# Making half of the second layer's modulation vectors in the token choice of the first expert layer instead of in the even mixer

## The chip, the cores and the metric

The program runs on one core of one Trainium2 chip. The metric is the device time of one execution in microseconds (us); the table further down gives the median of three runs. PE is TensorE with its matmuls, PEld its loading of weights, DVE VectorE, ACT ScalarE, POOL GpSimd and SP SyncE, whose queue issues most of the transfers. Numbers such as L926 are lines of the kernel before.

## What is computed

The reference is a first block (attention, gated recurrence, projections) and behind it two layers of a second block. Each layer of the second block needs six vectors per stream, made from a small input and one wide matrix, and ends in an expert layer that picks its tokens. Cut to what the change touches:

```python
for i in range(DEPTH_2):                                        # two layers
    mod = jnp.einsum('bd,de->be', jax.nn.silu(c), ada_w[i]) + ada_b[i]
    mod_c = jax.nn.silu(c_ctx) @ ada_w[i] + ada_b[i]
    sh1, sc1, g1, sh2, sc2, g2 = jnp.split(mod[:, None, :], 6, -1)
    ...
    h = rms_norm_2(x, norm1_g[i]) * (1.0 + sc1) + sh1           # norm 1
    y, yc = even_mixer(h, hc, ...)  if i % 2 == 0 else odd_mixer(h, hc, ...)
    x = x + g1 * y
    h = rms_norm_2(x, norm2_g[i]) * (1.0 + sc2) + sh2           # norm 2
    x = x + g2 * expert_choice_ffn(h, moe_router[i], moe_w1[i], moe_w3[i], moe_w2[i])

def expert_choice_ffn(h, router, w1, w3, w2):
    ...
    gate, idx = lax.top_k(jnp.swapaxes(aff, 1, 2), cap)         # 16 experts choose cap tokens each
    xs = jax.vmap(lambda hb, ib: hb[ib])(h, idx)
    hid = jax.nn.silu(jnp.einsum('becd,edf->becf', xs, w1)) * jnp.einsum('becd,edf->becf', xs, w3)
    ys = jnp.einsum('becf,efd->becd', hid, w2) * gate[..., None]
    ...                                                         # added back to the chosen rows
```

`x` has 512 rows and the context 256 rows of 1024 numbers; `ada_w` is 2 x 1024 x 6144, all in 32-bit floats.

## The kernel before

**The vectors.** `Mods.make(psum, p, w, ahead, part)` is a generator that makes the vectors of one layer. Part 0 makes `sh1` and `sc1`, part 1 the other four. It walks over pieces of `ada_w` of 512 rows by 128 columns. Each step of part 1, of which there are 64, loads one piece into a tile `aw` (256 KB, rows of 512 B; the load is L903, in a ring of `ahead` + 1 buffers) and multiplies it on PE (L926, four matmuls in the program, eight in the trace). After each eighth step ACT copies the sums (L931, tile `aev`), and one step later PE turns them (L910) and DVE adds the bias (L911). In front stand two small loads of the bias and the norm's gain into `aev` with a transpose (L240, L244), behind stand the gates' transposes (L942), a copy (L943) and a store (L944, to `mg`).

**The even mixer.** It starts with a gated stage (four column blocks, each of 512- and 256-column matmuls in three terms, L102 to L104, on weights that a `Feed` loads, splits on ACT into `whi` and on POOL into `wlo`, L184 to L201). Its results (`glu`, L1143 and L1144) feed a convolution of 31 taps per block. Three of the four blocks run on DVE, one instruction a tap (L1098, L1100, tile `acc`). Then come the low-rank projections: per row tile ACT squares (L1162), DVE and POOL make the norm (L110, L115), DVE scales (L1164), PE turns (L1178), ACT and DVE split (L1182, L1183). After them come attention and the output projection. The generator `both` is stepped between the matmuls of the gated stage and of the low-rank stage.

**The token choice.** `first.run()` is the expert layer of the first layer. Logits of all tokens lie in PSUM (L1517, L1518). `choose` turns them (L1534) and finds the largest eight per pass on DVE (L1544, L1545), eight passes for `x` and four for the context. Then it sums along the rows (L1550), turns (L1554), and `fetch` makes the list of rows (L1470, L1473). POOL gathers them (L1477, tile `xs`). `turn` (L1567) transposes the gathered rows, and with that the experts begin (L1617 up, L1656 down). The experts' weights arrive in 192 tiles `w` of 1 MB over a ring of 14. Eight are issued on SP before the choice, six on POOL behind the gather, the rest on SP as buffers come free.

**The order** of the instructions on each engine is fixed when the program is built: a scheduler orders what the generators emit, and each engine and each queue then works in that order.

Of the kernel before, what the change touches and what calls it, by code (L numbers as in the profile page):

```python
# [218 lines left out]
def setup(k):  # L219
    nc = k.nc  # L220
    k.cp = k.pool("cp", side="left")
    cc = k.cp.tile(list(CONSTS.shape), F32, name="cc")
    k.load_consts = lambda: nc.sync.dma_start(cc, k.i["consts"])
    k.c = {n: cc[:, o:o + w] for n, (o, w) in COFF.items()}
    k.id = k.c["ident"]
    k.mhalf = k.cp.tile([128, 1], F32, name="mhalf")
    nc.vector.memset(k.mhalf, -0.5)
# [631 lines left out]
def ada_setup(k, psum):  # L859

    nc, I = k.nc, k.i
    c1 = columns(k, [("c", I["c_2"].rearrange("a (r p) -> (a r) p", p=128)),
                     ("cc", I["c_ctx_2"].rearrange("(r p) -> r p", p=128))], k.cp, psum)
    k.router = k.cp.tile([128, 2, 8, 16], F32, name="router")
    for layer in range(2):
        nc.gpsimd.dma_start(k.router[:, layer], I["moe_router_2"][layer].rearrange("(k p) e -> p k e", p=128))
    k.cT = k.cp.tile([128, 8, 32], F32, name="cT")
    nc.gpsimd.memset(k.cT, 0.0)
    for r, nm in enumerate(("c", "cc")):
        th = k.cp.tile([128, 8], F32, name="cth" + nm)  # L870
        nc.scalar.activation(th, c1[nm], AF.Tanh, scale=0.5)
        nc.vector.scalar_tensor_tensor(th, th, 1.0, c1[nm], ALU.add, ALU.mult)
        nc.vector.tensor_scalar(k.cT[:, :, r], th, 0.5, None, ALU.mult)
# [558 lines left out]
def moe(k, layer, groups, mods, psum, es, nslot, extra, out=None, side="right"):  # L1432
# [19 lines left out]
    def load(upto, eng=nc.sync):  # L1452

        for i in range(len(W), min(upto, len(todo))):
            e, nm, q = todo[i]
            a = i % (nslot + extra) >= nslot
            w = pools[a].tile([128, 2 * D], F32, name="w", tag="w", bufs=extra if a else nslot).rearrange("p (k f) -> p k f", k=2)
            d = eng.dma_start(w, I[f"moe_{nm}_2"][layer, e][q * 256:q * 256 + 256].rearrange("(k p) f -> p k f", p=128))
            if i < nslot + extra:
                k.tc.keep_in_program_order(d)  # L1460
            W[e, nm, q] = w
# [211 lines left out]
                nc.scalar.copy(t[so], yb[64 * dh + 32:64 * dh + 64])  # L1673
                nc.vector.tensor_tensor(ys[so, ds_], ys[so, ds_], t[so], op=ALU.add)

    def run():
        nonlocal rp, pf, pq, p, iota, tid, one, hb
        slots()
        rp = k.pool(f"mr{layer}", 1, None, es)
# [10 lines left out]
        with ExitStack() as e2:  # L1690
            pq = k.pool(f"mq{layer}", 1, None, e2, "left")
            one = pq.tile([16, 512], F32, name="one")
            nc.gpsimd.memset(one, 1.0)
            chosen = [choose(gi, g) for gi, g in enumerate(G)]
            while any(g is None for g in nxt):
                for c in chosen:
                    next(c, 0)
        load(nslot + extra, nc.gpsimd)
        load(24)
        p = k.pool(f"mx{layer}", 1, None, es)  # L1700
# [879 lines left out]
def whole(tc, I, out):  # L2580
    nc = tc.nc
    with ExitStack() as es:
        k = K(tc, I, es)
        setup(k)
        psum = k.pool("ps", 8, PSUM)
        dr = k.pool("dr", 1, DRAM)
        mp = k.pool("mp", side="left")
        ex = ExitStack()
        mods = [Mods(k, i, mp, dr) for i in range(2)]

        def vectors():

            ada_setup(k, psum)
            with ExitStack() as e2:
                yield from mods[0].make(psum, k.pool("ad", 1, None, e2), 128, 4, 0)

        x = block1(k, lambda: k.pool("xp", 1, None, ex, "left").tile([128, 4, D], F32, name="xres"), psum, vectors)
        c = k.pool("xc", 1, None, ex, "left").tile([128, 2, D], F32, name="cres")
        nc.sync.dma_start(c, I["ctx_2"][0].rearrange("(t p) d -> p t d", p=128))
        xt, ct = [x[:, t] for t in range(4)], [c[:, t] for t in range(2)]  # L2600
        first = moe(k, 0, [(0, xt, 64), (1, ct, 32)], mods[0], psum, ExitStack(), 14, 0, side="left")
        def both(p):
            for a in range(2):
                yield from mods[1].make(psum, p, 128, 6, a)

        even_mixer(k, xt, ct, mods[0], psum, first, both)
        first.run()

        xs = dr.tile([S, D], F32, name="xspill")
        for t in range(4):  # L2610
            nc.sync.dma_start(xs[t * 128:t * 128 + 128], xt[t])

        def open_x():
            x2 = k.pool("xp2", 1, None, es, "left").tile([128, 4, D], F32, name="xres2")
            for t in range(4):
                nc.sync.dma_start(x2[:, t], xs[t * 128:t * 128 + 128])
            return [x2[:, t] for t in range(4)]

        res, last = [None] * 4, ExitStack()
        second = moe(k, 1, [(0, res, 64)], mods[1], psum, last, 11, 9, out[0])  # L2620
        odd_mixer(k, xt, ct, mods[1], psum, ex.close, open_x, second, last, res)
        second.run()
# [26 lines left out]
```

## Time and profile before

| | us |
|---|---|
| median of three runs | 3463.92 |
| lowest and highest of the three | 3454.38, 3468.79 |
| the profiled execution | 3452.15 |
| its span, from the first to the last instruction | 3450.3 |

The profiled execution is 12 us below the median. The span falls into stages, of which two matter here: the gated and low-rank stages of the even mixer, at 1020 to 1150 us, and the token choice of the first expert layer, at 1489 to 1523 us. A busy share is an average over stages with different limits, so each of the two is read by itself: which engine is full in it, and which wait ends last. The profile also gives, for any stretch, the clock that TensorE was granted (1.00 is 2.4 GHz, 0.50 is 1.2 GHz), the busy share of the 16 DMA engines (packets that overlap can bring it over 1) and the rate in GB/s.

### The profile page before, as it was taken

The numbers are of one execution on the slowest core, as the hardware profiler recorded it, in microseconds if no ns is written. First come the engines' busy times: TensorE is split into PE (matmuls) and PEld (weight loads), VectorE is DVE, ScalarE is ACT, GpSimd is POOL, SyncE is SP. The second block draws the span as 40 slices with busy tenths as digits, with TensorE's granted clock in tenths as the row PEclk, the third lists the DMA queues.
The fourth block names the chain that finished last, engine by engine and source line by source line (L and its number), as shares of the span: only waits on it lengthen the run. The fifth ranks groups of instructions, "written<-read, shape, count | busy, mean of one in ns | idle before, by whom it ended". The sixth has DMA issues, their size and how long they took to land.

```text
span 3450.3 us, 52389 instructions
## 1 busy us (share of the span) xinstructions
PE 3103.6 (90%) x21072; PEld 2032.6 (59%) x21072; DVE 1538.3 (45%) x3435; ACT 1013.0 (29%) x2175; POOL 975.3 (28%) x859
## 2 busy tenths in 40 slices
PE   8999999998989899979999999899768579699888
PEld 6898778886768666743333333687647467333322
DVE  3233544414378687342323334331577776332212
ACT  4333333322212454211111212222557443011000
POOL 5342434332323552410000000424646344000000
PEclk9999999999989999979999999899879779899999
DMA  4121122225257232178888884343222234799998
GB/s 145 61 74 49 62 74 70 66 68 166 93 158 203 81 101 65 49 304 339 333 341 334 333 339 166 105 140 117 80 59 71 66 96 154 311 409 409 409 409 349
DMA packets 372552, 625.94 MB, mean 181 GB/s; under 512 B 43998, under 2 KB 240525, under 8 KB 372310
## 3 DMA queue, kind: packets, MB, share of 16 engines
q1 hardware_dynamic: 367190, 603.58, 49.2%
q0 software_dynamic: 5120, 19.01, 1.5%
q8 instruction: 167, 2.74, 0.3%
q14 instruction: 75, 0.61, 0.1%
HBM read 596.61 MB, written 25.91 MB: 180 GB/s over the span
## 4 chain that ended last, share of the span: by engine, by line
PE 73%; DVE 11%; DMA 8%; ACT 4%; issue 2%; POOL 2%; SPq 1%; POOLq 0%; DVEq 0%; ACTq 0%
PE ps L102 11%; PE h L1617 10%; PE ps L103 10%; PE ps L104 10%; PE yb L1656 7%; DMA w<-in_moe_w_dram 6%; PE hc L1617 4%; PE ps L1599 2%; PE ps L926 1%; PE ob L762 1%; PE ps L2253 1%; DVE acc L1100 1%; DVE pr L2308 1%; DVE N L2309 1%; PE ob L1303 1%
## 5 line engine op out<-in xcount | busy, mean ns | idle before, releaser
L201 POOL TENSOR_TENSOR wlo<-wraw,whi 128x1024 fp32r<-128x1024 f32 (+5 forms) x219 | 426.8, 1970 | 755.2 <-ACT whi L197 736.5
L1617 PE MATMUL h<-w,xT 128*64 128x512 f32 x2048 | 462.6, 597 | 23.7 <-DMA w<-in_moe_w_dram 18.1
L1617 PEld LDWEIGHTS h<-w,xT 128*64 128x64 f32 x2048 | 141.1, 137 | 335.0 <-issue 253.9
L1656 PE MATMUL yb<-w,hT 128*64 128x512 f32 (+1 forms) x1536 | 301.0, 599 | 17.8 <-ACT hT L1640 15.4
L197 ACT CAST whi<-wraw 128x2048 fp32r<-128x2048 f32 (+4 forms) x108 | 161.5, 1495 | 235.7 <-PE ps L103 111.8
L1477 POOL DMA_INDIRECT xs<-xh,ii x20 | 21.3, 1067 | 728.9 <-DVE sl L1480 708.6
L1625 DVE SCALAR_TENSOR_TENSOR th<-th,h 128x512 f32<-128x512 f32 x32 | 22.0, 688 | 413.3 <-ACT th L1624 413.3
L1656 PEld LDWEIGHTS yb<-w,hT 128*64 128x64 f32 (+1 forms) x1536 | 87.2, 128 | 197.3 <-issue 153.6
L102 PE MATMUL ps<-hT,whi 128*128 128x512 f32 x416 | 171.2, 412 | 0.0
L102 PE MATMUL ps<-whi,hT 128*128 128x512 f32 (+1 forms) x424 | 164.3, 388 | 4.9 <-DVE hT L316 2.7
L103 PE MATMUL ps<-hT,wlo 128*128 128x512 f32 x416 | 166.3, 400 | 0.0
L1624 ACT ACTIVATE th<-h 128x512 f32<-128x512 f32 x32 | 19.1, 597 | 499.7 <-PE h L1617 499.7
L104 PE MATMUL ps<-hT,whi 128*128 128x512 f32 x416 | 165.7, 398 | 0.0
L103 PE MATMUL ps<-whi,hT 128*128 128x512 f32 (+1 forms) x424 | 156.4, 369 | 0.0
L104 PE MATMUL ps<-wlo,hT 128*128 128x512 f32 (+1 forms) x424 | 154.5, 367 | 0.0
L115 POOL TENSOR_TENSOR rs<-rs_t,mhalf 128x8 f32<-128x8 f32 (+3 forms) x78 | 94.7, 1218 | 113.5 <-DVE rs_t L110 93.7
L1617 PE MATMUL hc<-w,xT 128*32 128x512 f32 x1024 | 124.2, 598 | 0.0
L1669 DVE TENSOR_TENSOR ys<-yb,g 64x512 f32<-64x512 f32 x64 | 44.1, 688 | 177.5 <-PE yb L1656 177.0
L102 PEld LDWEIGHTS ps<-whi,hT 128*128 128x128 f32 x424 | 104.3, 246 | 14.5 <-DVE hT L316 3.2
L103 PEld LDWEIGHTS ps<-whi,hT 128*128 128x128 f32 x424 | 104.6, 247 | 6.4 <-issue 1.9
L1100 DVE SCALAR_TENSOR_TENSOR acc<-glu,w,acc 128x798 f32<-128x798 f32 x90 | 106.6, 1221 | 1.0
L104 PEld LDWEIGHTS ps<-wlo,hT 128*128 128x128 f32 x424 | 103.9, 246 | 5.2 <-issue 0.2
(810 smaller groups left out, 6831.4 us busy)
## 6 DMA issues: line engine op xcount, KB each, us to landing
w<-in_moe_w_dram SPq DMA_DIRECT2D x376, 1024.0 KB
wraw<-in_w_in_dram SPq DMA_DIRECT2D x48, 1024.0 KB
aw<-in_ada_w_dram SPq DMA_DIRECT2D x192, 256.0 KB
wraw<-in_od_w_in_dram SPq DMA_DIRECT2D x27, 512.0 KB
rows<-rw_rows SPq DMA_DIRECT2D x48, 192.0 KB
w<-in_moe_w_dram POOLq DMA_DIRECT2D x8, 1024.0 KB, 10.0
xh<-xn SPq DMA_DIRECT2D x10, 512.0 KB
wraw<-in_w_proj_b_dram SPq DMA_DIRECT2D x4, 1024.0 KB
```

Source lines behind the costliest of these rows:

```text
L102: nc.tensor.matmul(out, L[0], R[0], start=start, stop=False)
L103: nc.tensor.matmul(out, L[1], R[0], start=False, stop=False)
L104: nc.tensor.matmul(out, L[0], R[1], start=False, stop=stop)
L115: nc.gpsimd.tensor_tensor(out, t, mh.to_broadcast(list(ss.shape)), op=ALU.pow)
L197: nc.scalar.copy(hi, raw)
L201: eng.tensor_tensor(lo[:, a:b], raw[:, a:b], hi[:, a:b].bitcast(F32), op=ALU.subtract)
L762: nc.tensor.matmul(ob[pp, m * 128:m * 128 + 128], vs[a], pT[:, 2 * j + a], start=(a == 0), stop=(a == 1))
L1100: v.scalar_tensor_tensor(acc[:, c], glu[:, c, j:j + W], w2[:, j, c:c + 1], acc[:, c], ALU.mult, ALU.add)
L1599: nc.tensor.matmul(b, back, y[:, hs], start=(i == 0), stop=(i == len(terms) - 1))
L1617: nc.tensor.matmul(bb[o:o + cap], lhs, w[:, kk % 2, fh * 512:fh * 512 + 512], start=(kk == 0), stop=(kk == 7), tile_position=(0, o))
L1656: nc.tensor.matmul(yb[o:o + cap], lhs, w[:, j, dh * 512:dh * 512 + 512], start=first, stop=last, tile_position=(0, o))
L1669: nc.vector.tensor_tensor(ys[so, ds_], yb[64 * dh:64 * dh + 64], g["gate"][so, ds_], op=ALU.mult)
```

## The change

The even mixer now steps only part 0 of the second layer's `make` (32 steps). Part 1 (64 steps, second norm and gates) is given to `first.run` as a generator `more`. There it gets a pool of its own, is stepped five steps after each round of the two choosers, and is finished before the last six weight tiles are issued on POOL and before `turn`. Piece width and ring (`ahead` 6, thus seven buffers) are as before.

```diff
-    def run():
+    def run(more=None):
+
         nonlocal rp, pf, pq, p, iota, tid, one, hb
...
             nc.gpsimd.memset(one, 1.0)
+            other = Side(more(k.pool(f"mo{layer}", 1, None, e2))) if more else Side()
             chosen = [choose(gi, g) for gi, g in enumerate(G)]
             while any(g is None for g in nxt):
                 for c in chosen:
                     next(c, 0)
+                other.step(5)
+            other.drain()
         load(nslot + extra, nc.gpsimd)
         load(24)
...
-        def both(p):
-            for a in range(2):
-                yield from mods[1].make(psum, p, 128, 6, a)
-
-        even_mixer(k, xt, ct, mods[0], psum, first, both)
-        first.run()
+        even_mixer(k, xt, ct, mods[0], psum, first, lambda p: mods[1].make(psum, p, 128, 6, 0))
+        first.run(lambda p: mods[1].make(psum, p, 128, 6, 1))
```

What the scheduler makes of it follows for three engines; in these lists lines of the changed kernel lie up to four higher, and xN counts equal instructions in the program. On PE, in the token choice, before (`cum_13131` and `ext_13063` are those of `x`, the others of the context):

```order
L1534 MATMUL ps<-cc,aff_13037 16x128 x4
L1534 MATMUL ps<-cc,aff_13050 16x128 x2
L1554 MATMUL ps<-cc,cum_13100 128x16 x2
L1473 MATMUL ps<-ext_13077,oh 128x5 x2
L1554 MATMUL ps<-cc,cum_13131 128x16 x4
L1473 MATMUL ps<-ext_13063,oh 128x3 x4
L1567 MATMUL ps<-cc,xs 128x128 x16
```

On PE, the same place now, from the turn of `x` on (`cum_12992` and `ext_12639` are those of `x`):

```order
L926 MATMUL ps<-aw,cT 32x128 x4
L1554 MATMUL ps<-cc,cum_12992 128x16 x4
L926 MATMUL ps<-aw,cT 32x128 x16
L1473 MATMUL ps<-ext_12639,oh 128x3 x4
L926 MATMUL ps<-aw,cT 32x128 x12
L910 MATMUL ps<-cc,aev 128x2 x4
L926 MATMUL ps<-aw,cT 32x128 x32
L910 MATMUL ps<-cc,aev 128x2 x4
L926 MATMUL ps<-aw,cT 32x128 x32
L910 MATMUL ps<-cc,aev 128x2 x4
L942 MATMUL ps<-cc,mc_75 8x128 x2
L1567 MATMUL ps<-cc,xs 128x128 x16
```

Four matmuls are one step. 23 steps now stand ahead of the turn of the context, 41 ahead of the turn of `x`, 45 ahead of the row list of `x`, and all 64 ahead of the turn of the gathered rows.

On SP, from the end of the output projection on, before (`xh` is the store of normalised rows, `g_` a load of the gate row):

```order
L1506 DMA xh_12422<-xn 128x1024 x3
L950 DMA g_13009<-mg_74 128x1024
L950 DMA g_13011<-mg_74 128x1024
L1506 DMA xh_12422<-xn 128x1024
L1506 DMA xh_12436<-xn 128x1024 x2
L1458 DMA w<-in_moe_w_2_dram 128x2x1024 x186
```

On SP, the same place now, from the two small loads on:

```order
L240 DMA aev<-in_norm_g_dram 8x128
L903 DMA aw<-in_ada_w_dram 128x4x128
L1506 DMA xh_11949<-xn 128x1024
L903 DMA aw<-in_ada_w_dram 128x4x128 x5
L1506 DMA xh_11963<-xn 128x1024
L903 DMA aw<-in_ada_w_dram 128x4x128
L1506 DMA xh_11963<-xn 128x1024
L1458 DMA w<-in_moe_w_2_dram 128x2x1024 x8
L903 DMA aw<-in_ada_w_dram 128x4x128 x57
L944 DMA mg_80<-aev 8x4x128
L1458 DMA w<-in_moe_w_2_dram 128x2x1024 x178
```

Seven pieces now go ahead of the first eight weight tiles and 57 behind them.

On DVE, in the even mixer where the low-rank stage begins (`rs_t` is its first norm), before:

```order
L1100 SCALAR_TENSOR_TENSOR acc<-glu,w_7439,acc 128x798 x5
L911 TENSOR_TENSOR mc_75<-ps,pcol_b 128x8
L1100 SCALAR_TENSOR_TENSOR acc<-glu,w_7439,acc 128x798 x11
L911 TENSOR_TENSOR mc_75<-ps,pcol_b 128x8
L1100 SCALAR_TENSOR_TENSOR acc<-glu,w_7439,acc 128x798
L110 TENSOR_SCALAR rs_t<-lss 128x1
```

On DVE, the same place now:

```order
L1098 TENSOR_SCALAR acc<-glu,w_7439,pcol_qn 128x798
L1100 SCALAR_TENSOR_TENSOR acc<-glu,w_7439,acc 128x798 x11
L1143 SCALAR_TENSOR_TENSOR glu<-gl,ps 128x512
L1100 SCALAR_TENSOR_TENSOR acc<-glu,w_7439,acc 128x798 x2
L1144 SCALAR_TENSOR_TENSOR glu<-gl,ps 128x256
L1100 SCALAR_TENSOR_TENSOR acc<-glu,w_7439,acc 128x798 x14
L110 TENSOR_SCALAR rs_t<-lss 128x1
```

Of the 90 taps of L1100, 84 stood ahead of the first `rs_t` before, and 65 do now. The other 25 lie among the instructions of the low-rank stage; the number of taps is the same.

## Rows read from the trace of the kernel before

**Rows 1.** The page, busy time and share of the span by engine
```profile
PE 3103.6 (90%) x21072; PEld 2032.6 (59%) x21072; DVE 1538.3 (45%) x3435; ACT 1013.0 (29%) x2175; POOL 975.3 (28%) x859
```
**Rows 2.** Busy time by stretch: stretch, length, engines' busy us, clock, DMA share, GB/s
```profile
core 0: us, PE busy (x) PEld busy (x) DVE busy (x) ACT busy (x) POOL busy (x), PEclk, DMA share, GB/s
...
1020.00:1150.00 130.00, 117.68 (x1094) 97.61 (x1094) 103.32 (x168) 35.27 (x91) 44.67 (x52) 0.96 0.58 159
1470.00:1490.00 20.00, 19.16 (x122) 18.76 (x121) 5.37 (x13) 3.81 (x9) 1.24 (x4) 0.72 0.99 378
1490.00:1523.00 33.00, 8.44 (x40) 7.43 (x40) 23.92 (x74) 1.49 (x4) 7.56 (x14) 0.50 0.47 174
1523.00:1553.00 30.00, 30.00 (x164) 9.48 (x165) 5.22 (x14) 4.37 (x9) 1.26 (x1) 1.00 1.02 405
```
**Rows 3.** The same view, DVE's taps of line L1100 alone
```profile
1020.00:1150.00 130.00, 77.58 (x67) 0.96 0.58 159
```
**Rows 4.** The same view, matmuls of line L926 alone (the 64 steps)
```profile
1022.00:1140.00 118.00, 22.74 (x512) 11.86 (x512) 0.96 0.61 168
```
**Rows 5.** The same view, line L910 alone
```profile
1022.00:1140.00 118.00, 7.59 (x64) 8.07 (x64) 0.96 0.61 168
```
**Rows 6.** The chain that ended last, around one step: start, us, what
```profile
1057.73 0.24 PE ps L104
1057.97 0.36 PE ps L926 x8
1058.33 0.43 PE ps L102
1058.76 0.23 PE ps L103
```
**Rows 7.** Waits of 1015 to 1150: total us, times, longest
```profile
PE ps L244 <- DMA aev<-in_norm_g_dram: 6.3, 1, 6.3
```
**Rows 8.** DVE in time order, low-rank stage: start, us, what, idle before
```profile
1100.01 0.14 DVE L110 TENSOR_SCALAR rs_t<-lss 128x1 f32<-128x1 f32 x1
...
1133.34 0.15 DVE L110 TENSOR_SCALAR rs_t<-lss 128x1 f32<-128x1 f32 x1 [9.29 <-ACT lsq L1162]
```
**Rows 9.** PE in time order, token choice
```profile
1488.56 0.60 PE L1518 MATMUL lb<-rb,ones 1*128 1x16 f32 x2
1490.84 1.44 PE L1534 MATMUL ps<-cc,aff 128*16 128x128 f32 x6 [1.68 <-DVE mx L1530]
1503.90 0.36 PE L1554 MATMUL ps<-cc,cum 16*128 16x16 f32 x2 [11.62 <-DVE cum L1551]
...
1511.05 0.57 PE L1554 MATMUL ps<-cc,cum 16*128 16x16 f32 x4 [4.46 <-DVE cum L1551]
1512.76 1.84 PE L1473 MATMUL ps<-ext,oh 128*128 128x3 f32 x8 [1.13 <-DVE oh L1470]
1519.76 3.55 PE L1567 MATMUL ps<-cc,xs 128*128 128x128 f32 x16 [5.17 <-DMA xs<-xh,ii]
1523.24 1.94 PE L1617 MATMUL h<-w,xT 128*64 128x512 f32 x8
```
**Rows 10.** Busy time by stretch as in Rows 2, chosen for the DMA rate
```profile
1496.00:1498.00 2.00, 0.00 (x0) 0.00 (x0) 2.00 (x7) 0.00 (x0) 0.00 (x0) 0.50 0.75 293
1498.00:1508.00 10.00, 1.35 (x6) 1.21 (x6) 9.96 (x30) 0.00 (x0) 0.82 (x1) 0.50 0.00 1
1524.00:1540.00 16.00, 16.00 (x90) 4.76 (x88) 0.49 (x2) 1.50 (x4) 0.00 (x0) 1.00 1.02 408
1064.00:1068.00 4.00, 4.00 (x47) 3.22 (x40) 3.63 (x6) 1.05 (x2) 0.00 (x0) 1.00 1.22 291
```
**Rows 11.** SP's queue in time order, mixer and token choice
```profile
1058.50 0.37 SPq L184 DMA_DIRECT2D wraw<-in_ev_w_in_dram  x1
1058.96 15.75 SPq L903 DMA_DIRECT2D aw<-in_ada_w_dram  x13
...
1474.26 121.87 SPq L1458 DMA_DIRECT2D w<-in_moe_w_dram  x32
```
**Rows 12.** POOL in time order, token choice
```profile
1515.07 1.24 POOL L1477 DMA_INDIRECT xs<-xh,ii  x1 [6.77 <-DVE sl L1480]
1516.30 4.34 POOL L1458 DMA_DIRECT2D w<-in_moe_w_dram  x6
```

## The prediction

> **What bounds the kernel now.** First the page: PE is busy for 90% of the span [rows 1], so work taken from PE looks like time won. That share is an average, so I went on to the busy time of the two stretches that the change touches.
>
> In the even mixer's gated and low-rank stages, 130 us long, PE is busy for 117.7 us and DVE for 103.3 us [rows 2]. 77.6 us of DVE's time are taps of the convolution [rows 3]. Two engines are nearly full here. Relieving one helps until the other fills up.
>
> In the token choice the picture is reversed. From 1490 to 1523 us PE is busy for 8.4 of 33 us, at a granted clock of 0.50, which is 1.2 GHz, while DVE is busy for 23.9 [rows 2]. PE in order of time shows why: it waits 11.6 us for the sum of the context's list, 4.5 us for that of `x`, and 5.2 us for the gathered rows [rows 9]. The experts begin at 1523.24 us. So PE has room here. The DMA view tells what else has room: the engines are full up to about 1497.5 us (a share of 0.75 in the slice of 1496 to 1498) and stand still from 1498 to 1508 [rows 10]. Here is a gap of some 17 us up to the six weight tiles on POOL, which are issued from 1516.3 us [rows 12], and two gathers stand in it.
>
> **What the mixer gives back.** Removed are 64 steps. Their matmuls take 22.7 us of PE [rows 4] and the turns 7.6 us [rows 5]. A step that stands alone between other matmuls also delays the next one, which takes 0.43 us where its neighbour takes 0.23 [rows 6]. With some 40 such places this is 40 x 0.2 = 8 us, together 38 us. PE also loses its one wait of 6.3 us for the bias and gain [rows 7], together 45 us. That is the most that PE can give back.
>
> DVE sets a nearer bound. Of its 103.3 us only some 2.5 move away (eight bias additions, two scalings, two copies), so 100.8 us stay, and the stretch cannot become shorter than that: at most 130 - 100.8 = 29 us are won. The new order fits this. The first norm of the low-rank stage stood behind 84 taps and was reached at 1100.01 us [rows 8]; it now stands behind 65. The other 19 taps, at 77.58 / 67 = 1.16 us each 22 us of DVE, are not gone but stand between the norms of the low-rank stage. The holes that they fill are holes such as the 9.3 us before 1133 [rows 8].
>
> The lower end: only the part from 1111 to 1134, where DVE waited for PE, gets shorter for certain. Some 16 steps and three turns lie there, in pairs of about 0.77 us with the delay of the next matmul, and at 0.8 us each: 6.2 + 2.4 = 9 us. Between 9 and 29 I take 20, nearer to DVE's bound, since with that DVE would be busy for 92% of 110 us, as full as it was in much of the gated stage.
>
> **What the token choice pays.** All 64 steps stand ahead of the turn of the gathered rows on PE, and 45 of them ahead of the row list of `x`. PE's own part is small: 64 steps at 22.7 / 64 = 0.36 us, twice that at half the clock, fit beside the transfers. The pieces have to arrive first, though, and they have a rate of their own. In the mixer SP issued 13 of them in a row from 1058.96 us [rows 11], and while they flowed the DMA engines were past full (share 1.22) at 291 GB/s; weight tiles flow at 408 GB/s [rows 10]. A piece has 0.262 MB, so it takes 0.262 / 0.291 = 0.90 us.
>
> The sum, by the clock of the old trace:
> - The first eight weight tiles landed by 1497.5 us. Seven pieces go ahead of them: 7 x 0.90 = 6.3, thus 1503.8. (The first piece waits only for buffers that the output projection frees, and eight weight tiles behind it are off the path.)
> - 57 pieces follow: 57 x 0.90 = 51.3, thus 1555.1.
> - Two gathers of 0.52 MB each share the engines: 1.05 / 0.408 = 2.6, thus 1557.7.
> - The six weight tiles on POOL are issued behind the gather of `x`, which now waits for step 45, near 1503.8 + 38 x 0.90 = 1538. About 16 pieces are then still to come. The tiles need 6.29 / 0.408 = 15.4 us of the same engines. If the pieces go first they cost nothing, if the tiles go first all of it: 1557.7 to 1573.1.
> - After the last piece come its matmuls, the copy, the turn (about 2.5 us together) and the turn of the gathered rows, 3.55 us [rows 9]: 6 us.
>
> The experts then begin at 1563.7 to 1579.1 us, in place of 1523.2: 40.5 to 55.9 us later. Both queues have work at once and share the same engines, and then both end late, so I take 50.
>
> **What is hidden.** DVE's passes of the choice end near 1511 us and now wait for PE, not PE for them; they cost nothing more. The two small loads, eight copies on ACT and DVE's bias additions lie beside the transfers. On SP the remaining 178 weight tiles queue behind the 57 pieces and the store of the gates. The first of them needs the buffer of the first tile, which is free only when the experts have used it, so nobody waits for that. On POOL the gather waits for the list and the six tiles for the gather; both are in the sum. The expert stage itself is PE's: 30.00 of 30 us busy right after its start [rows 2], at a DMA share of 1.02. It begins, as before, with 14 tiles there or on the way. It moves as a whole, and its length stays.
>
> **The sum.** -20 + 50 = +30 us. From the profiled execution, 3452.2, this is 3482. The median of the runs shown lies 11.8 us above that execution, so the forecast for the median is 3464 + 30 = 3494. Ends of the terms: 40.5 - 29 = +11.5 and 55.9 - 9 = +47, thus 3475 to 3511.
>
> **The rivals.**
> - *PE bounds the mixer.* If the taps find room wherever PE's steps leave, the full 45 us come back, and -45 + 50 = +5: 3469, no change that can be measured. For it: PE has 117.7 busy us against DVE's 103.3. Against it: DVE's work that stays is 100.8 us, and it cannot run in 85. This decides if DVE could shift more than 15 us of its work out of the stretch; in the new order all taps of L1100 stay in it. 14 in 100.
> - *The pieces flow as fast as the weight tiles.* At 408 GB/s the 57 pieces take 57 x 0.64 = 36.6 us in place of 51.3: 14.7 less, +15, 3479. Against it: 291 GB/s at a share of 1.22 [rows 10], with the queue full. 8 in 100. Beside this stands a rule of the Trainium skill, "DMA: Bandwidth & Descriptors", section "Specifications": transfers reach line rate from 512 B on, and the pieces' rows have just that. By the rule this rival would hold; the row speaks against it, and I go by the row.
> - *The mixer gives back only its lower end*, because the low-rank chain through ACT, DVE, POOL and PE now has a tap between all its links: -9 + 50 = +41, 3505. 8 in 100.
> - *The change wins.* The choice would have to cost under 3 us at a gain of 20. The gap of 17 us without transfers is too short for 57 us of pieces. 4 in 100, for what I don't see.
>
> **How the numbers follow.** The forecast has the remaining 66 in 100. What a measurement of this kernel can tell from no change is about 0.5%, 17 us: slower means above 3481. The forecast's own range, 3475 to 3511, lies over that for nine parts in ten: 0.60, with 0.08 of the third rival and 0.01 of the second makes 0.69 for slower. 0.06 of the forecast, the first rival and most of the second make 0.26 for the same. 0.05 is left for faster. The range reaches down to the first rival, 3468, and up to the end of the terms, 3511.
>
> **What would show it.** In the changed trace: PE in the token choice waits on `aw` again and again; the DMA share is near 1 or above from 1470 us of the old clock to the experts' start, at about 290 GB/s once the first eight tiles are in; the gather of `x` is issued some 25 us later than before relative to the logits; the time from the last logits to the first L1617, 34 us now, is 75 to 90. In the mixer the time from 1020 to the end of the low-rank stage is 20 us shorter, with DVE over 90% busy and taps between the norms. I am wrong if the pieces arrive faster than 0.9 us each, if the mixer shrinks by 40 us, or if the expert stage changes its own length by more than 5 us.

## The result, and the profile of the changed kernel

The changed kernel takes 3499.2 us (median of four runs, 3496.0 to 3506.2); the kernel before, measured beside it, 3461.5. The ratio is 1.0111, 95% interval 1.0083 to 1.0139: 0.8 to 1.4% slower, as forecast (3494, range 3468 to 3511). The profiled execution of the changed kernel took 3495.96 us, 43.8 more than that of before; the medians are 37.7 apart, since the profiled execution of before was a quick one. What was moved is 64 of the 96 steps of the second layer, so two thirds and not half. One execution of a later kernel (24 steps in the choice) took 7601 us, more than twice any other; it is left out of the numbers, and with it the only trace of that kernel.

The page, busy time by engine, to be read against [rows 1]:

```profile
PE 3131.6 (90%) x21072; PEld 2055.6 (59%) x21072; DVE 1539.6 (44%) x3435; ACT 1012.2 (29%) x2175; POOL 983.2 (28%) x859
```

PE has exactly as many instructions as before and is busy for 28 us more; its mean granted clock is 0.934 where it was 0.945. The page shows nothing else; the two stretches have to be looked at.

**The mixer.** Busy time by stretch of the changed kernel (stretch, length, busy us of PE, PEld, DVE, ACT, POOL, clock, DMA share, GB/s), and below it the squares of line L1162, first of the kernel before, then of the changed one (count, durations in ns, first and last start):

```profile
1020.00:1100.00 80.00, 70.49 (x415) 65.67 (x414) 80.00 (x100) 19.89 (x45) 32.80 (x22) 0.94 0.19 55
```

```profile
L1162 ACT ACTIVATION_READ_ACCUMULATOR lsq<-ps x12: 194/196/217, 1095.5 to 1142.4; 128x1 f32 x12
```

```profile
L1162 ACT ACTIVATION_READ_ACCUMULATOR lsq<-ps x12: 191/200/225, 1070.8 to 1111.8; 128x1 f32 x12
```

DVE is busy for all 80 of 80 us: the bound that the prediction named. The last square of the low-rank rows comes 30.6 us sooner (1142.4, 1111.8). By the last of the turns that follow (L1178) it is 26.2 us (1145.3, 1119.1), and by the first scores of attention 29.2. DVE in order of time shows how the taps (L1100) now fill every hole between the norms' operations:

```profile
1092.15 1.04 DVE L1100 SCALAR_TENSOR_TENSOR acc<-glu,w,acc 128x798 f32<-128x798 f32 x1
1093.11 0.61 DVE L1183 SCALAR_TENSOR_TENSOR lr<-ps,pcol_qn,lr 128x128 fp32r<-128x128 f32 x2
1093.62 1.05 DVE L1100 SCALAR_TENSOR_TENSOR acc<-glu,w,acc 128x798 f32<-128x798 f32 x1
```

**Attention and output projection.** Their code is unchanged, but 8 of the 30.6 us are gone by the last logits (1489.2 before, 1466.6 after). First the two stretches of the kernel before, then those of the changed kernel:

```profile
1190.80:1387.70 196.90, 185.81 (x1495) 125.95 (x1495) 156.48 (x454) 110.92 (x298) 83.69 (x79) 0.95 0.28 83
1387.70:1489.20 101.50, 98.51 (x550) 83.06 (x548) 35.76 (x63) 25.33 (x43) 40.13 (x39) 0.95 0.33 122
```

```profile
1161.60:1361.10 199.50, 187.92 (x1496) 128.56 (x1496) 156.48 (x455) 111.03 (x298) 83.98 (x80) 0.94 0.27 81
1361.10:1466.60 105.50, 102.53 (x550) 86.68 (x548) 35.76 (x63) 25.35 (x43) 40.05 (x39) 0.91 0.35 125
```

In the second stretch PE's busy time times its granted clock is 98.51 x 0.95 = 93.6 before and 102.53 x 0.91 = 93.3 after: the same work at a lower clock. The two stretches together are 6.6 us longer. This is not shown to belong to the change: in the traces of seven experiments below whose mixer is that of the changed kernel, the last logits end between 1461.7 and 1473.9 us.

**The token choice.** From the end of the last logits to the first L1617 it took 1523.24 - 1489.16 = 34.1 us [rows 9] and now takes 94.9 (1466.60 to 1561.49). PE in order of time (start, us, what, and in brackets the wait before and what ended it), to be read against [rows 9]:

```profile
1466.00 0.60 PE L1518 MATMUL lb<-rb,ones 1*128 1x16 f32 x2
...
1469.93 3.21 PE L926 MATMUL ps<-aw,cT 128*32 128x128 f32 x56
1481.20 0.66 PE L926 MATMUL ps<-aw,cT 128*32 128x128 f32 x8 [8.06 <-DMA aw<-in_ada_w_dram]
...
1492.96 0.66 PE L926 MATMUL ps<-aw,cT 128*32 128x128 f32 x8 [0.24 <-DMA aw<-in_ada_w_dram]
1493.86 0.65 PE L926 MATMUL ps<-aw,cT 128*32 128x128 f32 x8 [0.24 <-DMA aw<-in_ada_w_dram]
...
1531.36 0.65 PE L926 MATMUL ps<-aw,cT 128*32 128x128 f32 x8 [4.19 <-DMA aw<-in_ada_w_dram]
1537.18 0.65 PE L926 MATMUL ps<-aw,cT 128*32 128x128 f32 x8 [5.17 <-DMA aw<-in_ada_w_dram]
1543.26 0.65 PE L926 MATMUL ps<-aw,cT 128*32 128x128 f32 x8 [5.42 <-DMA aw<-in_ada_w_dram]
...
1552.96 0.65 PE L926 MATMUL ps<-aw,cT 128*32 128x128 f32 x8 [0.17 <-DMA aw<-in_ada_w_dram]
1554.37 1.87 PE L910 MATMUL ps<-cc,aev 128*128 128x2 f32 x8 [0.76 <-ACT aev L931]
...
1561.49 3.65 PE L1617 MATMUL h<-w,xT 128*64 128x512 f32 x16 [1.23 <-DVE xT L1573]
```

The first seven steps find their pieces there, the eighth waits 8.06 us behind the eight weight tiles. After that a piece comes every 0.90 us, as at 1492.96 and 1493.86. Between 1531 and 1543 us one comes only every 5.8 us. PE's waits for pieces in the choice, in total us, times and longest:

```profile
PE ps L926 <- DMA aw<-in_ada_w_dram: 30.0, 22, 8.1
```

POOL in order of time shows what took the place of the pieces, and busy time by stretch shows the rates:

```profile
1522.12 4.34 POOL L1458 DMA_DIRECT2D w<-in_moe_w_dram  x6
```

```profile
1490.00:1500.00 10.00, 8.02 (x83) 4.81 (x82) 1.84 (x10) 0.58 (x1) 1.07 (x1) 0.58 1.15 293
1510.00:1520.00 10.00, 8.09 (x107) 5.24 (x100) 1.08 (x3) 0.59 (x1) 0.00 (x0) 0.67 1.03 274
1530.00:1540.00 10.00, 1.31 (x16) 0.40 (x16) 0.00 (x0) 0.00 (x0) 0.00 (x0) 0.50 1.04 395
```

While the six weight tiles on POOL and the pieces share the engines, 395 GB/s flow and PE is busy for 1.31 of 10 us. The pieces, though issued on a queue that had work before the tiles, get a small part of it. The DMA engines are full or nearly so up to the last piece (shares of 0.90 to 1.15 in stretches of 10 us).

**Behind it** 2 us are added in the experts' stage (the lag behind the kernel before is 38.2 us at their start and 40.2 at their end) and 3.3 in the second layer's mixer; with 0.3 at the end this makes the 43.8 of the two traces. Neither is shown to come from the change. The experts' stage, 611.7 us in the trace of before and 613.7 here, takes 619.2 and 619.4 in the traces of two variants of the kernel before further down (few taps, eight steps earlier). The quick execution of before was quick there.

### The profile page after: what moved, and what is told of

Its sections match the earlier page's. It is cut to its first block, busy times and chain, and to the rows that moved or that the text cites. A ratio compares the mean times of both kernels' runs of the same rounds, so it can differ in the third digit from the quotient of the medians.

```text
span 3494.1 us, 52398 instructions
## 1 busy us (share of the span) xinstructions
PE 3131.6 (90%) x21072; PEld 2055.6 (59%) x21072; DVE 1539.6 (44%) x3435; ACT 1012.2 (29%) x2175; POOL 983.2 (28%) x859
## 4 chain that ended last, share of the span: by engine, by line
PE 71%; DVE 13%; DMA 9%; ACT 4%; issue 2%; POOL 1%; SPq 1%; DVEq 0%; ACTq 0%; POOLq 0%
PE h L1617 10%; PE ps L102 10%; PE ps L103 10%; PE ps L104 10%; PE yb L1656 7%; DMA w<-in_moe_w_dram 5%; PE hc L1617 3%; DVE acc L1100 3%; DMA aw<-in_ada_w_dram 2%; PE ps L1599 2%; PE ps L926 1%; PE ps L2257 1%; PE ob L762 1%; DVE pr L2312 1%; DVE N L2313 1%
## 5 line engine op out<-in xcount | busy, mean ns | idle before, releaser
L1617 PE MATMUL h<-w,xT 128*64 128x512 f32 x2048 | 464.2, 599 | 23.7 <-DMA w<-in_moe_w_dram 17.0
L1617 PEld LDWEIGHTS h<-w,xT 128*64 128x64 f32 x2048 | 141.4, 137 | 335.5 <-issue 252.9
L1617 PE MATMUL hc<-w,xT 128*32 128x512 f32 x1024 | 123.1, 598 | 0.0
L926 PE MATMUL ps<-aw,cT 128*32 128x128 f32 x1536 | 86.2, 327 | 40.6 <-DMA aw<-in_ada_w_dram 37.5
L102 PEld LDWEIGHTS ps<-whi,hT 128*128 128x128 f32 x424 | 104.1, 245 | 14.6 <-DVE hT L316 3.2
L1100 DVE SCALAR_TENSOR_TENSOR acc<-glu,w,acc 128x798 f32<-128x798 f32 x90 | 109.4, 1252 | 0.6
```

The source lines that it names most:

```text
L102: nc.tensor.matmul(out, L[0], R[0], start=start, stop=False)
L926: nc.tensor.matmul(ps[32 * j:32 * j + 32, h * w:h * w + w], k.cT[:, 4 * q + j], raws[i][:, j], start=(q == 0), stop=(q == 1), tile_positio ...
L1100: v.scalar_tensor_tensor(acc[:, c], glu[:, c, j:j + W], w2[:, j, c:c + 1], acc[:, c], ALU.mult, ALU.add)
L1617: nc.tensor.matmul(bb[o:o + cap], lhs, w[:, kk % 2, fh * 512:fh * 512 + 512], start=(kk == 0), stop=(kk == 7), tile_position=(0, o))
```

## The experiments

All ratios are against the kernel before, run beside each. Where an edit moves lines, the line numbers in a trace lie a few higher than those of the kernel before.

**Without the loads.** The change: pieces 8 to 64 are not loaded (the lines inside `make` that do it are not shown).

```
-        first.run(lambda p: mods[1].make(psum, p, 128, 6, 1))
+        first.run(lambda p: mods[1].make(psum, p, 128, 6, 1, 7))   # only 7 loads, used in turn
```

> The changed kernel, but only the first seven pieces of part 1 are loaded; all 64 steps then multiply these seven, so this kernel leaves out 57 loads and its vectors are not the reference's. All steps, turns and gathers stay. Theory (the choice waits for the pieces in the queues): with nothing to wait for, the stretch from the last logits to the first expert multiplication, 34.1 us before and 94.9 after, falls to 34 to 50 us, and the kernel to 3430 to 3455 us, below the kernel before, since the mixer's gain (22.5 us at the last logits) stays. Rival (TensorE's own 64 steps, taken in turns with the choice and at half clock, set the stretch): it stays at 80 us or more, and the time within 15 us of the changed kernel's 3499.

Measured: 3455.3 us, ratio 0.9966 (0.9949 to 0.9984). PE in order of time (here L931 is L926 of before, L915 is L910, L1523 is L1518, L1622 is L1617):

```profile
1464.57 0.60 PE L1523 MATMUL lb<-rb,ones 1*128 1x16 f32 x2
...
1468.51 2.70 PE L931 MATMUL ps<-aw,cT 128*32 128x128 f32 x64
...
1495.54 3.64 PE L931 MATMUL ps<-aw,cT 128*32 128x128 f32 x64
1499.94 1.86 PE L915 MATMUL ps<-cc,aev 128*128 128x2 f32 x8 [0.76 <-ACT aev L936]
1501.73 1.93 PE L931 MATMUL ps<-aw,cT 128*32 128x128 f32 x32
1503.60 0.60 PE L1559 MATMUL ps<-cc,cum 16*128 16x16 f32 x4
...
1526.74 3.65 PE L1622 MATMUL h<-w,xT 128*64 128x512 f32 x16 [1.19 <-issue]
```

Nothing waits for a piece any more, and yet the stretch is 61.6 us (1465.17 to 1526.74), not 34. Both theories were too simple. The loads account for 94.9 - 61.6 = 33.3 us, near the 30.0 us for which PE waited for pieces above, and 27.5 remain that are PE's: a block of eight steps takes 3.64 + 0.76 + 1.86 = 6.2 us at half the clock. Three of the eight blocks lie beside DVE's passes and are free. Two and a half stand between the context's list and the turn of `x`'s sums (L1559; 1503.60, that is 38.4 us after the logits, in place of 21.9 before [rows 9]), and two and a half behind it. With all pieces at hand the move wins 0.3%: this is about the most that it could have brought in this order. The win stands in the medians alone. The traced execution, at 3464.1 us, is the longest of the five, and in it the experts begin 3.5 us later than in the trace of before.

**Part 1 divided** between mixer and choice, 24 or 32 steps in the choice:

```
+            yield from mods[1].make(psum, p, 128, 6, 1, range(4, 9))    # 40 steps in the mixer; or range(4, 8)
+        first.run(lambda p: mods[1].make(psum, p, 128, 6, 1, range(9, 12)))
```

> Part 1 divided: 40 of its 64 steps stay in the even mixer as in the kernel before, the last 24 (three of eight column blocks) go beside the choice. Theory (in the choice the steps cost twice: the first three blocks lie beside VectorE's passes, each further one takes about 6 us of TensorE at half clock, and pieces beyond the stretch in which the queues stand idle add their transfer): 24 steps fit, so the stretch from the last logits to the first expert multiplication is 34 to 42 us (34.1 before, 94.9 after); the mixer gives 24/64 of 45 us of TensorE, at most the 22 us that the whole move gave, so 8 to 17 us at the last logits; together 3450 to 3466 us against 3466, at best 15 us below the kernel before. Rival (any piece in the choice delays the queue of weights behind it, and the experts wait for it): the choice is as short, but the experts' stage grows by 10 us or more; 3466 to 3480.

> Part 1 divided half and half: 32 steps in the mixer, 32 beside the choice. Theory: one block more in the choice than there is cover for, 6 to 9 us on that stretch over the kernel with 24 steps there, against at most 5 us more from the mixer: 0 to 8 us slower than that kernel, 3454 to 3470. Rival (the choice has room for 32 steps): as fast or up to 5 us faster than with 24.

Measured: 3479.3 us with 24 (median of six; ratio 1.0053, 1.0034 to 1.0072), 3481.4 with 32 (1.0064, 1.0047 to 1.0081). Both theories were wrong by 11 us or more, and the two kernels are alike. The number with 24 lies in the range of its rival, but the rival's mechanism is not seen: with 32 steps the experts' stage takes 614.9 us, 3.2 more than in the trace of before and not 10. The trace of the kernel with 32 shows the low-rank squares and the choice:

```profile
L1164 ACT ACTIVATION_READ_ACCUMULATOR lsq<-ps x12: 193/194/209, 1092.9 to 1133.8; 128x1 f32 x12
```

```profile
1493.14 0.60 PE L1520 MATMUL lb<-rb,ones 1*128 1x16 f32 x2
...
1533.26 1.86 PE L910 MATMUL ps<-cc,aev 128*128 128x2 f32 x8 [0.76 <-ACT aev L931]
...
1535.50 0.61 PE L1556 MATMUL ps<-cc,cum 16*128 16x16 f32 x4
...
1544.28 3.48 PE L1569 MATMUL ps<-cc,xs 128*128 128x128 f32 x16 [5.20 <-DMA xs<-xh,ii]
1547.68 4.51 PE L1619 MATMUL h<-w,xT 128*64 128x512 f32 x20
```

The mixer gives 8.6 us (1142.4 to 1133.8) and the choice takes 53.9, 20 more than before, with half the steps. PE's queue shows why: the turn of `x`'s sums (L1556 here) stands behind all 32 steps, 41.8 us after the logits in place of 21.9, and only then come the list, the gather with its 5.20 us and the transposes. Some 11 of these 41.8 us are waits for pieces, 7.66 of them before the eighth. The 8.6 us of the mixer do not reach the choice in this trace: the last logits end 4.6 us later than in that of before (1493.74 against 1489.16), after an attention of 209.2 us where it had 196.9 (see the last experiment). Even a few steps on an idle engine are not free if the chain has a short link on that engine behind them.

**DVE's taps cut** from 31 to 15, in both kernels, to test the bound of the mixer:

```
-        for j in range(31):
+        for j in range(15):
```

> The kernel before with VectorE's taps of the convolution cut from 31 to 15; it leaves out the other taps, so its output is not the reference's. It is one half of a pair, with the changed kernel cut the same way. Theory (VectorE bounds the mixer's stretch at 1020 to 1110 us once TensorE's steps are gone, and in the kernel before both are near their limit): the kernel before gains little in this stretch by fewer taps, 0 to 15 us at the last square of the low-rank rows (1142.4 us with all taps), since TensorE still has its 45 us of steps there. Rival (VectorE bounds it in the kernel before already): 25 us or more.

> The changed kernel with VectorE's taps cut from 31 to 15 (leaves out the other taps). Theory (VectorE's bound is what kept the mixer's gain at 30.6 us at the last square of the low-rank rows, of TensorE's 45): here VectorE is out of the way, so the gain at that place, against the kernel before with as few taps, is 38 to 45 us, and VectorE is busy under 80% of 1020 to 1100 us. Rival (something else keeps it, TensorE's clock or the order of the steps): 31 us or less.

The low-rank squares, first of the kernel before with few taps, then of the changed one:

```profile
L1162 ACT ACTIVATION_READ_ACCUMULATOR lsq<-ps x12: 193/194/215, 1093.4 to 1138.5; 128x1 f32 x12
```

```profile
L1162 ACT ACTIVATION_READ_ACCUMULATOR lsq<-ps x12: 193/196/209, 1068.1 to 1100.0; 128x1 f32 x12
```

In the kernel before, half the taps bring 3.9 us (1142.4 to 1138.5): there PE holds the stage. With few taps the move gives 38.5 us (1138.5 to 1100.0) in place of 30.6. Busy time of the changed kernel with few taps shows DVE out of the way and PE full:

```profile
1020.00:1100.00 80.00, 77.02 (x489) 72.39 (x488) 48.05 (x87) 26.39 (x69) 33.73 (x43) 1.00 0.20 57
```

So DVE's taps are what kept the gain below PE's 38 to 45, as the theory says. PE gains in two ways that this pair does not part: it waits less, and its granted clock in this stretch is 1.00 in place of 0.94. There is one execution of each kernel, 3459.9 and 3488.5 us.

**Wider pieces**, 256 columns, so rows of 1 KB:

```
-        first.run(lambda p: mods[1].make(psum, p, 128, 6, 1))
+        first.run(lambda p: mods[1].make(psum, p, 256, 3, 1))
```

> The changed kernel, but part 1 in 32 pieces of 512 rows by 256 columns (rows of 1 KB, 3 ahead) in place of 64 pieces with rows of 512 bytes: the same bytes. Theory A (the length of a row sets the 291 GB/s at which pieces come): the rate goes towards the 390 to 408 GB/s of the weight tiles, so 15 MB take 37 to 42 us in place of 51, and the first expert multiplication comes 8 to 14 us sooner; 3485 to 3491 us. Theory B (something else sets it, so the rate stays at about 291 GB/s): within 4 us of 3499.

Measured: 3492.9 us, 1.0066 (1.0041 to 1.0092); the stretch is 81.4 us (1473.86 to 1555.30). That is between the theories, and the trace shows a second cause that neither names. Busy time by stretch and POOL's issue of the six tiles:

```profile
1500.00:1510.00 10.00, 5.95 (x56) 1.89 (x48) 0.17 (x1) 0.58 (x1) 0.00 (x0) 0.67 0.99 314
1530.00:1540.00 10.00, 6.72 (x52) 3.29 (x48) 0.17 (x1) 0.58 (x1) 0.00 (x0) 0.50 0.68 218
```

```profile
1548.45 4.33 POOL L1458 DMA_DIRECT2D w<-in_moe_w_dram  x6
```

The rate is 314 GB/s at a share of 0.99, where the changed kernel had 274 to 293 at shares above 1, and in slices of 2 us with a share above 1.05 it is 346 to 365. So longer rows do come faster, as theory A has it, but with at most four pieces under way the queues are not always full (218 at 0.68). The second cause is that here the gather, and behind it the six tiles, were issued after the last piece. The gaps of 5.8 us are gone, and 13.5 us with them. The two effects were not parted.

**The six tiles behind the pieces**, tried in two ways: on SP, and on POOL behind a copy of a finished vector.

```
-        load(nslot + extra, nc.gpsimd)
+        load(nslot + extra, nc.sync if more else nc.gpsimd)
```

```
+        if more:
+            k.tc.keep_in_program_order(nc.gpsimd.tensor_copy(rp.tile([128, 8], F32, name="seen"), mods_next.A[1, 1]))
         load(nslot + extra, nc.gpsimd)
```

> The changed kernel, but the six expert weight tiles that GpSimd issues at the end of the choice are issued by SyncE behind the 57 pieces. Theory (the six tiles of 1 MB go ahead of the pieces that still stand in the queue and take their whole 15.4 us from them): the gaps of 4 to 6 us between pieces at 1526 to 1545 us vanish, all pieces come about 0.9 us apart, and the first expert multiplication comes 10 to 15 us sooner; the time falls to 3484 to 3490 us, if the experts do not miss the tiles, which they reach over 60 us later. Rival (the queue as a whole carries what it carries, and the tiles are missed later): the first expert is sooner, but an expert waits as much longer, and the time stays within 4 us of 3499.

> The changed kernel, but GpSimd first copies one of part 1's finished vectors (128 by 8), so that its six weight tiles are issued only when the last piece has come; this is what the kernel e2_tiles_behind was meant to be, where the scheduler had put the tiles ahead of 16 pieces again. Theory (the tiles take their whole 15.4 us from the pieces): the waits of 4 to 6 us for a piece are gone, the stretch from the last logits to the first expert multiplication falls from 94.9 to 78 to 85 us, and since the second weight of the first expert is needed over 20 us after that, the time falls to 3484 to 3491. Rival (the first expert then waits for these tiles): the time stays within 4 us of 3499.

Measured: 3497.6 us (1.0098, 1.0082 to 1.0115) and 3495.7 (1.0097, 1.0077 to 1.0117). Neither did what it was written for, so neither shows the choice with the tiles out of the way. SP's queue and one wait of PE in the first, POOL's queue in the second:

```profile
1519.84 4.25 SPq L903 DMA_DIRECT2D aw<-in_ada_w_dram  x4
1524.18 4.03 SPq L1458 DMA_DIRECT2D w<-in_moe_w_dram  x4
1528.30 8.98 SPq L903 DMA_DIRECT2D aw<-in_ada_w_dram  x3
```

```profile
1542.77 0.66 PE L926 MATMUL ps<-aw,cT 128*32 128x128 f32 x8 [10.56 <-DMA aw<-in_ada_w_dram]
```

```profile
1523.81 0.19 POOL L1703 COPY seen<-mA 128x8 f32<-128x8 f32 x1 [3.26 <-DVE mA L936]
1524.31 4.30 POOL L1458 DMA_DIRECT2D w<-in_moe_w_dram  x6 [0.32 <-issue]
```

In the first the scheduler put the tiles between the pieces again, ahead of the last 16, 12 and 9 of them. There the four tiles in a row cost one wait of 10.56 us, so tiles that stand ahead in the same queue cost the pieces about as much as tiles on POOL. In the second the vector that the copy waits for was made from blocks five and six of eight and was ready at 1523.8 us, with 16 pieces still to come. What the tiles' overtaking costs is thus read from traces in which it happens, and not from one without it: in the changed kernel three waits of 4.19, 5.17 and 5.42 us, together 14.8.

**More loaded ahead.** Fifteen pieces ahead of the weight tiles; and, in a second form, three blocks loaded whole into free weight slots, 13 pieces more ahead, and 39 steps given out in the first turn (23 calls, in which each of the six wide pieces counts for four steps); and this form with the copy of above:

```
-        first.run(lambda p: mods[1].make(psum, p, 128, 6, 1))
+        first.run(lambda p: mods[1].make(psum, p, 128, 14, 1))
```

```
+        for c in (range(4, 4 + 3) if more else ()):
+            for q in range(2):
+                own.append(pools[0].tile([128, 2 * D], F32, name="w", tag="w", bufs=nslot).rearrange("p (k c) -> p k c", k=4))
+                nc.sync.dma_start(own[-1], I["ada_w_2"][1][q * 512:q * 512 + 512, c * 512:c * 512 + 512].rearrange("(k p) c -> p k c", p=128))
...
-                other.step(5)
+                other.step(next(paces, 0))      # 23, 0, 0, 0, 0, 8
```

> The changed kernel with 15 pieces loaded ahead of the weight tiles in place of 7; nothing else. Theory (the order in the queue matters only as far as TensorE's first wait: the eighth piece came 8 us late behind the weight tiles): that wait of 8 us goes, but the bytes are the same, so the stretch falls by 0 to 8 us; 3490 to 3500. Rival (what was queued ahead of the pieces is all of the loss): by 15 us or more; under 3485.

> All 64 steps stay in the choice, but the pieces come earlier and in another order: three of the eight column blocks are loaded whole (6 pieces of 1 MB, rows of 2 KB) into the six weight slots that are filled last, ahead of the eight first weight tiles; 13 pieces of the other blocks are loaded ahead as well; 39 of 64 steps are given out in the choice's first turn, beside VectorE's passes. Theory (two costs in the choice: the pieces' transfer, and TensorE's steps at half clock, between which the choice's own small steps stand in line; without loads the stretch was 61.5 us, with them 94.9): the stretch from the last logits to the first expert multiplication falls to 45 to 60 us, the time to 3445 to 3465 us, that is level with the kernel before or up to 15 us faster. Rival (the queues still bound it: 31 MB from 1443 us on at 300 to 400 GB/s last until 1520 to 1545 us, whatever the order): the stretch stays at 75 us or more, or the first experts wait for weights; 3475 to 3495.

> The kernel q1_slots (39 steps in the first turn, pieces loaded early into free weight slots) with the six weight tiles held back in the same way. Theory: the stretch of 87 us there loses the three waits of 5 us, 70 to 76 us remain; 3478 to 3488. It stays slower than the kernel before, since 16.8 MB of pieces at about 300 GB/s need 55 us, of which the queues had 17 us free in the choice and some 10 us before it. Rival (without the tiles' overtaking the choice is bound by TensorE alone, as in e1_no_loads): 61 us, 3462 or less.

Measured: 3496.0 us (1.0102, 1.0086 to 1.0117), 3500.2 (1.0105, 1.0083 to 1.0127) and 3488.6 (1.0073, 1.0053 to 1.0093). With fifteen ahead the stretch is 94.0 us, as its theory had it: the wait of 8 us became one of 12 before the sixteenth piece. In the second form it is 87.0, in the third 85.3; the copy again waited too early (POOL issued at 1512.96 us), so the third kernel does not test its theory either. Busy time by stretch of the second form:

```profile
1444.00:1544.00 100.00, 66.18 (x579) 46.50 (x576) 31.20 (x94) 9.68 (x18) 10.38 (x22) 0.60 1.05 352
1476.00:1480.00 4.00, 2.97 (x13) 1.24 (x14) 4.00 (x12) 0.58 (x1) 0.00 (x0) 0.50 1.05 391
1480.00:1490.00 10.00, 9.24 (x88) 5.92 (x92) 6.03 (x14) 0.58 (x1) 0.00 (x0) 0.50 1.02 409
1530.00:1540.00 10.00, 0.65 (x8) 0.20 (x8) 0.00 (x0) 0.00 (x0) 0.00 (x0) 0.50 1.04 387
```

and of the changed kernel:

```profile
1444.00:1553.00 109.00, 71.86 (x718) 54.60 (x719) 30.59 (x92) 9.04 (x17) 9.71 (x21) 0.56 1.02 321
```

The engines are full in both. 64 pieces, eight tiles and six tiles are 16.8 + 8.4 + 6.3 = 31.5 MB; with the stores and gathers beside them 35.2 MB pass in 100 us in the second form, and 35.0 MB in 109 us in the changed kernel. The rival expectation held for the stretch: the bytes and their rate set the end, the order hardly. The time of 3500.2 us, 5 beyond the rival's range, did not follow the shorter stretch.

**Eight steps earlier in the kernel before**, where PE idles ahead of the first convolution matmul:

```
         other.add(beside(k.pool("evb", 1, None, el2)))
+        other.step(9)
```

> The kernel before, with the first 8 of the mixer's 96 steps given out before the first convolution multiplication, where TensorE stands idle for some 16 us between 935 and 960 us and the first seven pieces land by about 951 us. Theory (TensorE bounds the mixer of the kernel before, as the few-taps pair says): the steps cost nothing there, 8 times 0.45 to 0.65 us, so 3 to 6 us are won at the last square of the low-rank rows; 3455 to 3461 against 3462. Rival (VectorE's passes, which begin no sooner, or the convolution's first weights, now behind seven pieces, hold it): within 2 us of the kernel before, or up to 6 us slower.

Measured: 3465.7 us, 1.0001 (0.9988 to 1.0015). In its trace the last low-rank square comes 5.7 us sooner (1136.7), as the theory says, but the time doesn't follow. In the traced execution attention ran at a lower clock and took 211.3 us, against 196.9 at 0.95 in the kernel before:

```profile
1183.20:1394.50 211.30, 195.76 (x1512) 133.00 (x1511) 157.29 (x459) 112.26 (x300) 83.15 (x80) 0.89 0.26 77
```

The kernel with 32 steps in the choice had the same in its trace: 209.2 us at 0.91, and the same 1512 matmuls in place of 1495.

```profile
1181.30:1390.50 209.20, 192.73 (x1512) 130.76 (x1511) 156.74 (x459) 112.31 (x300) 83.08 (x80) 0.91 0.26 78
```

In both, two more steps (16 matmuls of L926) fall into attention, and PE waits once 4.5 us for DVE where it waited 0.5 in the kernel before. So a part of the loss lies in the order of the instructions. The clock alone can add as much: the trace with wider pieces has 206.1 us at 0.90 with 1495 matmuls. How much of a gain in the mixer is given back there stays open. No kernel of this study that makes all its loads is faster than the kernel before.

## Why the prediction was right, and where it was lucky

- **The mixer** was to give 20 us, with DVE's bound at 29. It gave 30.6 at the last square, 26.2 at the last turn of the low-rank rows and 29.2 at the start of attention: the taps filled every hole, and the bound was reached and not 92% of it. The step that chose 20 between 9 and 29 was too careful; the mechanism (DVE takes over from PE) is shown by the pair with few taps. At the last logits only 22.6 were left, 6.6 of the loss being a lower granted clock, which differs between executions. So the term of 20 fits the end of the stage before the choice by luck.
- **The rate.** Seven pieces and eight tiles were to be in 1503.8 - 1489.2 = 14.6 us after the logits, the eighth piece 0.9 later; it was multiplied at 1481.20 - 1466.60 = 14.6. From there to the last piece 56 x 0.90 + 2.6 = 53.0 us were forecast; 71.8 were measured, and without 14.8 for the tiles 57.0. At 0.90 us a piece (293 GB/s at best, 274 later) the rival of 408 GB/s is out. By the Trainium skill, "DMA: Bandwidth & Descriptors", section "Specifications", rows of 512 B would be enough for line rate; here they gave 274 to 293 GB/s, rows of 1 KB at most 365, rows of 2 KB 391, and tiles with rows of 4 KB 409.
- **The tiles** were given some 10 of their 15.4 us, on the view that both queues end late. They went ahead and took 14.8. While both were open a piece came every 5.8 us, 0.262 / 5.8 = 45 of the 395 GB/s; the tiles had the other 350, a ratio of 7.8. The Trainium skill, "DMA: Bandwidth & Descriptors", section "Queues, rings and completion order", says that an engine takes its queues in turn, a whole packet of several descriptors from each. If a packet holds as many rows of either kind, rows of 4 KB and of 512 B share as 8 to 1, which the 7.8 fits. No run here shows a packet or two queues with other rows, so this stays an explanation that fits one figure.
- **The tail** was 8.5 us (1552.96 to 1561.49) where 6 were forecast. With some 4 more for the pieces, 5 for the tiles and 2.5 for the tail, less 0.9 at the eighth piece, the stretch grew by 60.8, above the upper bound of 55.9. That bound was too low. The whole sum stayed inside its range because the mixer gave 22.6 by the last logits, and not the 9 with which the upper end was made.
- **PE's part** was called small and hidden. Hidden it was for the most part, behind the transfers. Small it was not: by the prediction's own figures it is 64 x 0.72 = 46 us, longer than the whole choice before, and the wait for the copy and the turn of each block, 0.76 + 1.86 us, are not in it. Without any load 27.5 us of the 60.8 stay. This step failed, though it cost the forecast nothing. A reader who had removed the transfers by this sum would have expected 34 us and found 61.6.
- **The experts' stage** kept its length within 2 us, as forecast (under 5).
- **The signs**: DVE at 100% with taps between the norms, `aw` waited for 22 times, the gather of `x` issued at 1520.89 us, 54.3 after the logits in place of 25.9, all as written. The stretch of 94.9 lies beyond the 75 to 90 that were written.

The sum was +30; the medians say +37.7. The choice was 10.8 us more than forecast, the mixer 2.6 better at the logits, and the later stages 5 us longer, which makes 43 for the traces; the difference to the medians' 37.7 is the quick execution of before. The last 5 us were not forecast, and they lie within what two traces differ by.

## What to carry to other kernels

Before work is moved to a stretch where an engine idles, ask of three things and not of one: its bytes against what the queues have free there, its place in that engine's queue ahead of the short links of the chain, and its duration at the clock that an idle engine is granted. Here the matmuls of a step took 0.36 us in the busy stage; in the idle one a step took 6.2 / 8 = 0.78 us with its copy and turn, and 0.90 us when its piece had to arrive. And where a second engine is nearly as full as the one that is relieved, its busy time is the bound of the gain, and it can be reached in full.

## What the runs showed of the hardware

- PE's granted clock falls to half (1.2 GHz) while PE is busy all the time: in the logits, where matmuls of 16 columns stand among turns of 128, it is 1.00 from 1440 to 1450 us and 0.50 from 1460 on. In the choice stretches of 10 us have 0.50 to 0.67, and from 1560 us, in the experts, it is 1.00 again. The stretch of the fall in the changed kernel:

```profile
1450.00:1460.00 10.00, 10.00 (x50) 9.87 (x49) 2.08 (x3) 1.17 (x2) 0.00 (x0) 0.53 1.07 354
```

- Executions of one kernel differ by the clock that they are granted. Of 45 executions of the kernel before, the 13 with a mean clock of 0.938 or 0.939 have spans of 3461.2 to 3467.1 us, the seven with 0.943 to 0.945 spans of 3449.6 to 3460.0. The experts' stage took 611.7 to 619.4 us in traces of kernels that are alike there. A difference of 5 us between two single traces in a PE-bound stage is thus no finding.
- Loads came faster with longer rows while the engines were full: 274 to 293 GB/s with 512 B, 346 to 365 with 1 KB, 391 with 2 KB (the wide pieces, 1476 to 1480 us) and 409 with 4 KB.
- Two queues with rows of different lengths do not share the engines evenly: 1 MB tiles with rows of 4 KB took some 350 of 395 GB/s while pieces with rows of 512 B, on the queue that had been at work before, came at a sixth of their pace alone.
